# A split-precision encoder kernel on one core: the two parts of the activations put side by side in one tile

## Chip, core and metric

The kernel runs on one core of a Trainium2 chip. The metric is the device time of one execution in microseconds (us). "PE" is the matmul engine, "DVE" the vector engine, "ACT" the scalar engine, "POOL" GpSimd, "SP" the engine that here only issues DMAs.

## What is computed

Two residual layers over 256 tokens of width 2048, batch 1, float32 throughout. Cut to what matters:

```python
for layer in range(2):
    h = rms_norm(x, g[0])
    if layer % 2 == 0:                       # "even"
        proj = h @ even_w_in                 # GLA q, k, v, gate, 32 low-rank columns; neighbourhood attention q, k, v
        o = concat(gla_mixer(...), na_mixer(...))
        mix = o @ even_w_out
    else:                                    # "odd"
        proj = h @ odd_w_in                  # SSD z, x/B/C, 32 dt columns; sliding-window q, k, v
        o = concat(ssd_mixer(...), swa_mixer(...))
        mix = o @ odd_w_out
    x = x + rms_norm(mix, g[1])
    h = rms_norm(x, g[2])
    x = x + rms_norm((silu(h @ w_gate) * (h @ w_up)) @ w_down, g[3])
```

## The kernel before

**Split products.** Each float32 operand is split into a rounded part (hi, type fp32r) and the rest (lo). A product is then three matmuls: hi by hi, hi by lo, lo by hi; lo by lo is left out. Weights arrive over SP's DMA queue as halves of a chunk (`raw`, 128x1024, five buffers); for each half ACT makes `whi` (L184) and DVE makes `wlo` (L186), seven buffers each. The activations of a norm are transposed and split by `begin_norm` into four pairs of tiles `xth`, `xtl`, each 128 x 4 x 256 (four slices of the contraction, 256 tokens).

**Two kinds of product.** `unit_a` (L198) gives outputs with tokens on the partitions: activations are loaded into the array and 512 weight columns are streamed, 24 matmuls of 512 columns for a chunk and 128 tokens. `unit_b` (L233) gives transposed outputs: 128 weight columns are loaded, and the 256 tokens are streamed, 16 contraction steps of three matmuls of 256 columns. The even layer has 24 such units (GLA q and k: 8; attention q and k: 16), the odd layer 12 (the channels of the convolution, `conv`), and each layer one more of kind "L", for the 32 low-rank or dt columns: these stand in columns 0 to 15 and 32 to 47 of an otherwise zero chunk. The result of a unit stays in one of four PSUM tiles (`accb`) until a DVE multiplication by the row of norm factors (`mul_row`, L690 or L692) takes it out; L745 does so for the even layer's "L" unit, L1113 for the odd one's.

**What runs beside the units.** Mixers are generators (`spawn`, `tick`) that are stepped while the projections run. In the even layer `gla` turns the low-rank result `lrT` into decays (`gz`, L795) and then, for seven levels, forms `ge` on DVE and ACT, multiplies it (L845) and has PE make scores from it (`gs`, L821); DVE merges them (L851). The order of the instructions on each engine is set at compile time by the framework's scheduler; every engine then goes through its list in order.

**Memory.** Most 4 KB tiles come from one pool, `s4`, with 26 buffers: `xth` and `xtl` take 8 of them, the rest goes to residuals, mixer tiles, and, in the FFN, to the weights of its second product (`sw`, by SP's queue) and combinations of activations (`so`). The FFN's second product is done in fewer matmuls by adding weights and activations first (`quads`, L555; sums by L567; matmuls `sq`, L618 to L620). Before the end of each half layer, `post` has POOL load the residual `x` (L635) and the gains `gb` (L371).

Of the kernel before, what the change touches and what calls it, by code (L numbers as in the profile page):

```python
# [18 lines left out]
F32 = mybir.dt.float32  # L19
F32R = mybir.dt.float32r  # L20
# [19 lines left out]
PREP = 200  # L40
# [51 lines left out]
class Trunk:  # L92
    def __init__(self, tc, dr, out, stage=99):
        self.tc, self.nc, self.dr, self.out, self.stage = tc, tc.nc, dr, out, stage
        self.plan = []
        self.pending = deque()
        self.bg = []
        self.early = deque()
        self.hooks, self.mid = deque(), deque()
        self.lag = 2 * LAG  # L100
        self.nraw = 0
        self.rate, self.width, self.credit = 1.0, 3, 0.0
        self.n = 0
        self.pinned = {}
        self.pinning = ()
        self.ready = deque()
        self.tight = False
        self.splan, self.sraw, self.squeue = [], {}, deque()


# [50 lines left out]
    def chunk(self, kind, name, idx, k0, n0):  # L161

        if self.hooks and len(self.plan) == self.hooks[0][0]:
            self.hooks.popleft()[1]()
        self.plan.append((kind, name, idx, k0, n0))
        while len(self.ready) < 2:
            self.prep()
        n = 2 if kind == "A" else 8
        return [tuple(v.rearrange("p (k n) -> p k n", k=n) for v in self.ready.popleft()) for _ in range(2)]

    def prep(self):

        while len(self.early) < 4 and self.nraw < 2 * NCHUNK:
            self.load_half()
        if not self.early:
            return
        self.ready.append(self.halves(self.early.popleft()))

    def halves(self, src):

# [17 lines left out]
    def unit_a(self, chunks, xk, evac):  # L198

        nc = self.nc  # L200
        last = len(chunks) - 1
        ps = {}

        def part(t, ci, w, kt0, half):
            if ci == 0 and half == 0:
                ps[t] = self.pacc.tile([P, 512], F32, tag="acc", name=self.nm("acc"))
            for k in (2 * half, 2 * half + 1):
                wh, wl = w[half]
                xh, xl = xk(kt0 + k, t)
                s, e = ci == 0 and k == 0, ci == last and k == 3  # L210
                self.pin(nc.tensor.matmul(ps[t], xh, wh[:, k % 2], start=s, stop=False))  # L211
                self.pin(nc.tensor.matmul(ps[t], xh, wl[:, k % 2], start=False, stop=False))  # L212
                self.pin(nc.tensor.matmul(ps[t], xl, wh[:, k % 2], start=False, stop=e))  # L213
            if ci == last and half:
                evac(t, ps[t])
            self.tick(0.5)

        if self.tight:
            self.flush()
        for ci, (name, idx, k0, n0, kt0) in enumerate(chunks):  # L220
            w = self.chunk("A", name, idx, k0, n0)
            if self.tight:
                for half in range(2):
                    part(0, ci, w, kt0, half)
                    part(1, ci, w, kt0, half)
                continue
            for half in range(2):
                part(0, ci, w, kt0, half)
                if self.mid:
                    self.mid.popleft()()  # L230
            self.push(*(lambda h=h, ci=ci, w=w, kt0=kt0: part(1, ci, w, kt0, h) for h in range(2)))

    def unit_b(self, name, idx, n0, xt, kind="B"):  # L233

# [70 lines left out]
    def begin_norm(self, li, gi):  # L305

        nc = self.nc
        xt = ([None] * 4, [None] * 4)
        rs = [None, None]
        ssp = [None, None]  # L310
        gain = self.gT[:, li * 2 + gi // 2]

        def piece(t, j, src):
            if xt[0][j] is None:
                xt[0][j], xt[1][j] = self.slot([P, 4, T], F32R, "xth"), self.slot([P, 4, T], F32R, "xtl")
            if j == 0:
                ssp[t] = self.small([P, 4], "nss", "nss")
                rs[t] = self.keep.tile([P, 1], F32, tag="nrs", bufs=4, name=self.nm("nrs"))
            sl = slice(t * P, (t + 1) * P)
            hi, lo = xt[0][j][:, :, sl], xt[1][j][:, :, sl]  # L320
            with self.tc.high_priority(offset=NORM):
                ps = self.transpose4(src)
            yield
            with self.tc.high_priority(offset=NORM):
                gx = self.tmp([P, 4, P], nm="gx")
                self.pin(nc.vector.tensor_tensor(out=gx, in0=ps, in1=gain[:, 4 * j:4 * j + 4].unsqueeze(2)
                                                 .broadcast_to([P, 4, P]), op=ALU.mult))
                self.pin(nc.scalar.copy(hi, gx))  # L328
# [325 lines left out]
    def setup(self, ctx):  # L654
        nc, tc, dr = self.nc, self.tc, self.dr
        pool = lambda name, bufs, **k: ctx.enter_context(tc.tile_pool(name=name, bufs=bufs, **k))
        self.const = pool("const", 1)
        self.keep = pool("keep", 2)
        self.smp = pool("small", 8)
        self.raw = pool("raw", 5)  # L660
        self.whi = pool("whi", 7)
        self.wlo = pool("wlo", 7)
        self.s4 = pool("s4", 26)
        self.t2 = pool("t2", 4)
        self.t2m = pool("t2m", 6)
        self.junk = pool("junk", 1)
        self.pacc = pool("pacc", 4, space=PSUM)
        self.pmx = pool("pmx", 4, space=PSUM)
        self.dram = pool("dram", 1, space=bass.MemoryType.DRAM)
        self.xsrc = [self.dr["x"][t * P:(t + 1) * P] for t in range(2)]  # L670
        self.mhalf = self.const.tile([P, 1], F32, name="mhalf")
        nc.gpsimd.memset(self.mhalf, -0.5)
        self.load_const("ca", nc.scalar)
        self.x = [[None, None], [None, None]]
        self.load_x(0, 0, nc.sync)
        self.load_half()
        self.load_half()
# [47 lines left out]
    def even_mixers(self, norm, after):  # L725
        nc = self.nc
        self.have = {}
        self.in_xt, self.in_rs, _ = norm
        xt, w = self.in_xt, "even_w_in"
# [11 lines left out]
        nc.vector.tensor_copy(self.lv, lv)  # L741
        row = self.rstd_rows(self.in_rs)
        lrT = self.keep.tile([48, T], F32, tag="lrT", bufs=1, name="lrT")
        ps = self.unit_b(w, 0, 3072, xt, "L")
        nc.vector.tensor_mul(lrT, ps[0:48], row[0:48])  # L745
        for half in range(2):
            self.spawn(self.gla(half, lrT, mix))
        for half in range(2):
            t = self.slot([P, 2, 2, T], nm="gqk")
            for j in range(2):  # L750
                c0 = (2 * half + j) * P
                self.mul_row(t[:, 1, j], self.unit_b(w, 0, 512 + c0, xt), row)
                self.mul_row(t[:, 0, j], self.unit_b(w, 0, c0, xt), row, 0.125)
            self.have[f"qk{half}"] = t
        self.nat_unit(w, 1024, "gv0")
        self.nat_unit(w, 1024 + 512, "gv1")
# [1 line left out]
        for u in range(2):  # L758
            nq, nk = self.slot([P, 4, T], nm="nq"), self.slot([P, 4, T], nm="nk")
            for h in range(4):  # L760
                c0 = (4 * u + h) * P
                back = lambda x: x.rearrange("p (a t) -> p a t", a=2)[:, :, ::-1]
                self.mul_row(nq[:, h].rearrange("p (a t) -> p a t", a=2), back(self.unit_b(w, 0, 3104 + c0, xt)),
                             back(row), P ** -0.5)
                self.mul_row(nk[:, h], self.unit_b(w, 0, 4128 + c0, xt), row)
            self.nat_unit(w, 5152 + 512 * u, f"nv{u}")
            self.flush()
            self.new_mix(mix, 2 + u)
# [235 lines left out]
    def odd_mixers(self, norm, after):  # L1004
# [20 lines left out]
        self.unit_a([(w, 0, 512 * c, 3616, 4 * c) for c in range(4)], xk, ev_kv)  # L1025
        self.flush()
        row = self.rstd_rows(rs)
        ps = self.unit_b(w, 0, 2560, xt, "L")
        self.spawn(self.ssd_dt(ps, row))
        ssp = [self.small([P, 2], "yss", "yss") for _ in range(2)]  # L1030
        for g in range(2):
            bc = self.mtmp([P, 2, T], nm="bc")
# [68 lines left out]
            yield  # L1101
        return end

    def ssd_dt(self, ps, row):

        nc = self.nc
        R = 48

        def tl(nm):
            return self.mtmp([R, 2, T], nm=nm)  # L1110
        xu = tl("dx")
        x, u = xu[:, 0], xu[:, 1]
        nc.vector.tensor_mul(x, ps[0:R], row[0:R])  # L1113
        nc.scalar.activation(u, x, AF.Abs, bias=self.dtb[0:R])
        dt = self.keep.tile([R, T], F32, tag="lrT", bufs=1, name="dtk")
        nc.vector.tensor_scalar(out=dt, in0=x, scalar1=self.dtb[0:R], scalar2=0.0, op0=ALU.add, op1=ALU.max)
# [275 lines left out]
```

## Time and profile before

| | |
|---|---|
| time before, median of 3 runs | 2235.45 us (2234.25 to 2236.69) |
| the profiled execution's own time | 2236.18 us |
| its span in the profile | 2234.4 us, so 1.8 us lie outside |
| PE busy | 2189.1 us, 98% of the span |
| DVE busy | 1773.0 us |
| ACT busy | 1212.1 us |

A busy share is the union of an engine's instructions. A matmul's duration holds the time that its result needs to come out of the array, and the next one starts before that; how fast PE goes is read from the starts of neighbours, not from the durations.

### The profile page before, as it was taken

To read this page: it belongs to the slowest core of one execution; us is meant where nothing else is said; L and a number is where in the kernel's file an instruction comes from. 1 tells how busy PE (TensorE), PEld (TensorE's weight loads), DVE (VectorE), ACT (ScalarE), POOL (GpSimd) and SP (SyncE) were. 2 spreads that over 40 slices of the span, in tenths; PEclk is the share of its full clock that TensorE was granted. 3 is DMA by queue.
4 is the path that set the end of the run, shared out by engine and by line. 5 is a ranking of instruction groups with operands and counts; after the bars stand their busy time and mean duration, and the time that the engine had idled before them with its cause. 6 is when DMAs were issued, how large, how long until landed. Compare 5 with 4: busy or idle time off the path is not lost.

```text
span 2234.4 us, 29039 instructions
## 1 busy us (share of the span) xinstructions
PE 2189.1 (98%) x10888; PEld 1843.0 (82%) x10888; DVE 1773.0 (79%) x2134; ACT 1212.1 (54%) x1511; POOL 201.3 (9%) x246
## 2 busy tenths in 40 slices
PE   8999999999999999999989999999999999999997
PEld 7989998788888888888769988877888888888875
DVE  7877545766878888888989987766687889888896
ACT  6545345554555555555656545655556555555563
POOL 0001010210000000000021253121000000000002
PEclk9999999999999999999999999999999999999998
DMA  7445556575575655565656433657466565546563
GB/s 280 133 132 167 188 183 193 185 244 167 202 243 173 211 173 199 169 217 198 210 183 217 158 121 124 218 189 264 152 205 235 181 212 176 201 161 209 198 213 117
DMA packets 117325, 424.54 MB, mean 190 GB/s; under 512 B 13392, under 2 KB 13520, under 8 KB 117184
## 3 DMA queue, kind: packets, MB, share of 16 engines
q1 hardware_dynamic: 110592, 400.61, 53.4%
q0 software_dynamic: 6448, 21.99, 3.0%
q8 instruction: 85, 1.39, 0.2%
q14 instruction: 56, 0.46, 0.1%
q10 hardware_dynamic: 144, 0.10, 0.0%
HBM read 414.25 MB, written 8.39 MB: 189 GB/s over the span
## 4 chain that ended last, share of the span: by engine, by line
PE 88%; DVE 9%; issue 2%; DMA 1%; ACT 0%; POOL 0%; DVEq 0%; SPq 0%; ACTq 0%; POOLq 0%
PE acc L213 19%; PE acc L211 19%; PE acc L212 19%; PE sq L618 5%; PE sq L619 5%; PE sq L620 5%; DVE wlo L186 4%; PE accb L242 3%; PE accb L244 3%; PE accb L243 3%; DVE sw L567 1%; PE tp L285 1%; PE gs L821 1%; DVE f L627 1%; PE as L946 1%
## 5 line engine op out<-in xcount | busy, mean ns | idle before, releaser
L186 DVE TENSOR_TENSOR wlo<-raw,whi 128x1024 fp32r<-128x1024 f32 x596 | 741.7, 1252 | 292.4 <-ACT whi L184 284.5
L184 ACT CAST whi<-raw 128x1024 fp32r<-128x1024 f32 x596 | 624.5, 1051 | 580.6 <-PE acc L213 387.7
L213 PE MATMUL acc<-whi,xtl 128*128 128x512 f32 x1760 | 691.8, 394 | 6.0 <-DVE xtl L331 5.9
L212 PE MATMUL acc<-wlo,xth 128*128 128x512 f32 x1760 | 689.8, 393 | 0.6 <-DVE wlo L186 0.6
L211 PE MATMUL acc<-whi,xth 128*128 128x512 f32 x1760 | 677.3, 394 | 3.6 <-ACT xth L328 3.5
L184 ACT CAST whi<-sw 128x1024 fp32r<-128x1024 f32 x280 | 293.3, 1053 | 231.4 <-PE acc L213 132.6
L213 PEld LDWEIGHTS acc<-whi,xtl 128*128 128x128 f32 x1760 | 332.7, 189 | 77.6 <-DVE xtl L331 8.7
L211 PEld LDWEIGHTS acc<-whi,xth 128*128 128x128 f32 x1760 | 332.6, 189 | 73.9 <-ACT xth L328 5.4
L212 PEld LDWEIGHTS acc<-wlo,xth 128*128 128x128 f32 x1760 | 332.8, 189 | 70.8 <-DVE wlo L186 1.7
L186 DVE TENSOR_TENSOR wlo<-sw,whi 128x1024 fp32r<-128x1024 f32 x280 | 337.8, 1220 | 47.7 <-ACT whi L184 44.9
L619 PE MATMUL sq<-wlo,so 128*128 128x512 f32 x560 | 220.0, 393 | 4.5 <-DVE wlo L186 4.5
L620 PE MATMUL sq<-whi,so 128*128 128x512 f32 x560 | 219.2, 391 | 0.0
L618 PE MATMUL sq<-whi,so 128*128 128x512 f32 x560 | 219.2, 394 | 0.0
L567 DVE TENSOR_TENSOR sw<-sw,sw 128x1024 f32<-128x1024 f32 x160 | 193.8, 1220 | 17.9 <-DMA sw<-sstream 17.4
L242 PE MATMUL accb<-xth,whi 128*128 128x256 f32 x608 | 173.8, 286 | 0.0
L244 PE MATMUL accb<-xth,wlo 128*128 128x256 f32 x608 | 173.0, 285 | 0.0
L243 PE MATMUL accb<-xtl,whi 128*128 128x256 f32 x608 | 172.8, 284 | 0.0
L619 PEld LDWEIGHTS sq<-wlo,so 128*128 128x128 f32 x560 | 106.0, 189 | 28.6 <-DVE wlo L186 7.0
L620 PEld LDWEIGHTS sq<-whi,so 128*128 128x128 f32 x560 | 106.0, 189 | 22.5 <-DVE so L536 0.6
L618 PEld LDWEIGHTS sq<-whi,so 128*128 128x128 f32 x560 | 106.0, 189 | 22.2 <-ACT whi L184 0.4
L635 POOL DMA_DIRECT2D x<-xm x8 | 4.3, 544 | 1291.9 <-ACT whi L184 645.5
L242 PEld LDWEIGHTS accb<-xth,whi 128*128 128x128 f32 x608 | 116.5, 192 | 1.6 <-issue 0.7
(245 smaller groups left out, 2254.2 us busy)
## 6 DMA issues: line engine op xcount, KB each, us to landing
raw<-wstream SPq DMA_DIRECT2D x596, 512.0 KB, 4.9
sw<-sstream SPq DMA_DIRECT2D x160, 512.0 KB, 6.3
gb<-norm_gains POOLq DMA_DIRECT2D x16, 256.0 KB, 7.8
xm<-x POOLq DMA_DIRECT2D x16, 256.0 KB, 3.4
x<-xm POOLq DMA_DIRECT2D x8, 512.0 KB, 5.4
x<-x SPq DMA_DIRECT2D x4, 512.0 KB, 8.9
x<-x POOLq DMA_DIRECT2D x4, 512.0 KB, 7.7
xf<-x POOLq DMA_DIRECT2D x8, 256.0 KB, 3.2
```

The lines of the kernel that those rows point to most:

```text
L184: self.pin(nc.scalar.copy(hi, src))
L186: self.pin(nc.vector.tensor_sub(lo, src, hi.bitcast(F32)))
L211: self.pin(nc.tensor.matmul(ps[t], xh, wh[:, k % 2], start=s, stop=False))
L212: self.pin(nc.tensor.matmul(ps[t], xh, wl[:, k % 2], start=False, stop=False))
L213: self.pin(nc.tensor.matmul(ps[t], xl, wh[:, k % 2], start=False, stop=e))
L242: nc.tensor.matmul(ps, wh[:, kt % 8], xh, start=kt == 0, stop=False)
L243: nc.tensor.matmul(ps, wh[:, kt % 8], xl, start=False, stop=False)
L244: nc.tensor.matmul(ps, wl[:, kt % 8], xh, start=False, stop=kt == 15)
L567: nc.vector.tensor_add(a, a, b)
L618: nc.tensor.matmul(ps, xh, wh[:, k], start=s, stop=False)
L619: nc.tensor.matmul(ps, xh, wl[:, k], start=False, stop=False)
L620: nc.tensor.matmul(ps, xl, wh[:, k], start=False, stop=e)
```

## The change

The two parts of the activations become the two halves of one 8 KB tile, from a pool `s8` with four buffers; `s4` shrinks from 26 to 18 buffers. The even layer's 24 units become `unit_b2`: the product of `whi` with hi and with lo is one matmul of 512 columns, whose moving operand is two runs of 256 columns, 4 KB apart; the product of `wlo` with hi stays a matmul of 256 columns that adds into the first half. At the end ACT copies the second half out and DVE adds the first half to it, and the multiplication by the row follows. The odd layer's 12 units stay as they are. In the two "L" units the low parts of the 48 used columns are written into columns 64 to 111 of `whi` itself (`lhalf`), so that one matmul of 512 columns for each contraction step gives all products; two ACT copies, two DVE additions and the multiplication take the result out.

```diff
+LHALF = (9, 10, 323, 324)
...
+    def lhalf(self, src):
...
+            hi = self.whi.tile([P, 1024], F32R, tag="whi", name=self.nm("whi"))
+            self.pin(nc.scalar.copy(hi, src))
+            k, r = (v.rearrange("p (k n) -> p k n", k=8) for v in (hi, src))
+            self.pin(nc.vector.tensor_sub(k[:, :, 64:112], r[:, :, 0:48], k[:, :, 0:48].bitcast(F32)))
+        return hi, hi
...
+    def joined(self, kt, xt):
+        return xt[2][kt // 4][:, :, kt % 4, :]
+
+    def unit_b2(self, name, n0, xt):
...
+        ps = self.pacc.tile([P, 2, T], F32, tag="acc", name=self.nm("acc2"))
+        for kt in range(16):
+            wh, wl = w[kt // 8]
+            wide = lambda s, e: nc.tensor.matmul(ps, wh[:, kt % 8], self.joined(kt, xt), start=s, stop=e)
+            if kt < 15:
+                wide(kt == 0, False)
+            nc.tensor.matmul(ps[:, 0], wl[:, kt % 8], xt[0][kt // 4][:, kt % 4, :], start=False, stop=False)
+            if kt == 15:
+                wide(False, True)
...
+        t = self.tmp([P, T], nm="half")
+        nc.scalar.copy(t, ps[:, 1])
+        nc.vector.tensor_add(t, ps[:, 0], t)
+        return t
+
+    def unit_l(self, name, n0, xt, out, row):
...
+        for kt in range(16):
+            nc.tensor.matmul(ps, w[kt // 8][0][:, kt % 8], self.joined(kt, xt), start=kt == 0, stop=kt == 15)
...
+        t = self.tmp([48, 2, T], nm="lt")
+        nc.scalar.copy(t[:, 0], ps[0:48, 1])
+        nc.scalar.copy(t[:, 1], ps[64:112, 0])
+        nc.vector.tensor_add(t[:, 0], ps[0:48, 0], t[:, 0])
+        nc.vector.tensor_add(t[:, 0], t[:, 0], t[:, 1])
+        nc.vector.tensor_mul(out, t[:, 0], row[0:48])
...
-                xt[0][j], xt[1][j] = self.slot([P, 4, T], F32R, "xth"), self.slot([P, 4, T], F32R, "xtl")
+                xt[2][j] = self.s8.tile([P, 2, 4, T], F32R, tag="s8", name=self.nm("xt"))
+                xt[0][j], xt[1][j] = xt[2][j][:, 0], xt[2][j][:, 1]
...
-        self.s4 = pool("s4", 26)
+        self.s4 = pool("s4", 18)
+        self.s8 = pool("s8", 4)
...
-        ps = self.unit_b(w, 0, 3072, xt, "L")
-        nc.vector.tensor_mul(lrT, ps[0:48], row[0:48])
+        self.unit_l(w, 3072, xt, lrT, row)
...
-                self.mul_row(t[:, 1, j], self.unit_b(w, 0, 512 + c0, xt), row)
-                self.mul_row(t[:, 0, j], self.unit_b(w, 0, c0, xt), row, 0.125)
+                self.mul_row(t[:, 1, j], self.unit_b2(w, 512 + c0, xt), row)
+                self.mul_row(t[:, 0, j], self.unit_b2(w, c0, xt), row, 0.125)
```

PE, in a unit of the even layer's GLA q and k; `accb_474` is the unit's PSUM tile, each row one matmul. Before:

```order
L242 MATMUL accb_474<-xth_115,whi_464 128x256
L243 MATMUL accb_474<-xtl_116,whi_464 128x256
L244 MATMUL accb_474<-xth_115,wlo_466 128x256
L242 MATMUL accb_474<-xth_124,whi_464 128x256
L243 MATMUL accb_474<-xtl_125,whi_464 128x256
L244 MATMUL accb_474<-xth_124,wlo_466 128x256
```

Now, with `acc_94_444` the unit's tile, and `rb` the small matmuls that spread the norm factors:

```order
L257 MATMUL acc_94_444<-xt_126,whi_434 128x512
L260 MATMUL acc_94_444<-xt_126,wlo_436 128x256
L257 MATMUL acc_94_444<-xt_126,whi_434 128x512
L260 MATMUL acc_94_444<-xt_126,wlo_436 128x256
L401 MATMUL rb_389<-dg_390,ones 128x128
L401 MATMUL rb_389<-dg_393,ones 128x128
```

Three matmuls of a contraction step have become two, a wide and a narrow one by turns.

DVE, right behind the even layer's "L" unit: the norm row is copied, the low-rank result taken out, and weights and the first unit follow. Before:

```order
L346 COPY rstdB_389<-rb_390 128x256
L745 TENSOR_TENSOR lrT<-accb_411,rstdB_389 48x256
L186 TENSOR_TENSOR wlo_696<-raw_568,whi_694 128x1024
L186 TENSOR_TENSOR wlo_702<-raw_630,whi_700 128x1024
L798 TENSOR_SCALAR gm_499<-gz_501,cb_380 128x256
```

Now:

```order
L284 TENSOR_TENSOR lt_425<-accl_408,lt_425 48x256
L402 COPY rstdB_388<-rb_389 128x256
L285 TENSOR_TENSOR lt_425<-lt_425 48x256
L199 TENSOR_TENSOR wlo_633<-raw_574,whi_631 128x1024
L286 TENSOR_TENSOR lrT<-lt_425,rstdB_388 48x256
L199 TENSOR_TENSOR wlo_677<-raw_580,whi_675 128x1024
L267 TENSOR_TENSOR half_515<-acc_94_444,half_515 128x256
L199 TENSOR_TENSOR wlo_683<-raw_623,whi_681 128x1024
L854 TENSOR_SCALAR gm_461<-gz_463,cb_379 128x256
```

The low-rank result now needs three DVE instructions, with a `wlo` between them, and the addition of the first unit's halves stands ahead of the decays `gm`.

PE, where the scores of the second and third level of the first GLA half stand (`gs`, from `ge`). Before, inside the last q and k unit:

```order
L821 MATMUL gs_905<-ge_874 128x128 x4
L821 MATMUL gs_910<-ge_874 128x128 x4
L242 MATMUL accb_1011<-xth_115,whi_1001 128x256
L243 MATMUL accb_1011<-xtl_116,whi_1001 128x256
L244 MATMUL accb_1011<-xth_115,wlo_1003 128x256
L242 MATMUL accb_1011<-xth_115,whi_1001 128x256
L243 MATMUL accb_1011<-xtl_116,whi_1001 128x256
L821 MATMUL gs_986<-ge_955 128x128 x4
L821 MATMUL gs_991<-ge_955 128x128 x4
```

Now, behind that unit, in the projection for `gv0`:

```order
L226 MATMUL acc_958<-whi_992,xt_126 128x512
L877 MATMUL gs_794<-ge_771 128x128 x4
L877 MATMUL gs_799<-ge_771 128x128 x4
L877 MATMUL gs_862<-ge_839 128x128 x4
L877 MATMUL gs_867<-ge_839 128x128 x4
L224 MATMUL acc_958<-whi_992,xt_126 128x512
```

The scores have moved behind more of the projections. SP's list of DMAs is the same before and now, and PE's list in the FFN too.

## Rows read from the trace of the kernel before

**Rows 1.** The page: busy time, share and count by engine; PE's granted clock in 40 slices.

```profile
PE 2189.1 (98%) x10888; PEld 1843.0 (82%) x10888; DVE 1773.0 (79%) x2134; ACT 1212.1 (54%) x1511; POOL 201.3 (9%) x246
...
PEclk9999999999999999999999999999999999999998
```

**Rows 2.** The chain that ended last, shares by engine.

```profile
PE 88%; DVE 9%; issue 2%; DMA 1%; ACT 0%; POOL 0%; DVEq 0%; SPq 0%; ACTq 0%; POOLq 0%
```

**Rows 3.** Stretches: start:end us, length, busy us (count) by engine, clock, DMA.

```profile
47.00:130.00 83.00, 83.00 (x599) 74.92 (x598) 71.02 (x112) 48.46 (x56) 0.00 (x0) 1.00 0.39 125
...
1060.00:1100.00 40.00, 39.53 (x171) 31.45 (x170) 40.00 (x46) 23.22 (x26) 0.00 (x0) 1.00 0.63 209
```

**Rows 4.** Groups by line: count | busy us, mean ns | idle before, releaser.

```profile
L242 PE MATMUL accb<-xth,whi 128*128 128x256 f32 x608 | 173.8, 286 | 0.0
...
L821 PE MATMUL gs<-ge 64*128 64x128 f32 x256 | 24.9, 285 | 0.0
```

**Rows 5.** PE's timeline in a 256-column unit: start us, duration; 51 starts apart.

```profile
59.82 0.28 PE L244 MATMUL accb<-xth,wlo 128*128 128x256 f32 x1
...
65.94 0.28 PE L244 MATMUL accb<-xth,wlo 128*128 128x256 f32 x1
```

**Rows 6.** PE's timeline in a stretch of 512-column matmuls; 56 starts apart.

```profile
1699.70 0.39 PE L618 MATMUL sq<-whi,so 128*128 128x512 f32 x1
...
1712.40 0.39 PE L620 MATMUL sq<-whi,so 128*128 128x512 f32 x1
```

**Rows 7.** Groups by line, ACT and DVE: reads of 256 PSUM columns, weight halves.

```profile
L980 ACT CAST mixh<-apo 128x256 fp32r<-128x256 f32 x16 | 5.9, 372 | 10.0 <-PE apo L979 10.0
L981 DVE TENSOR_TENSOR mixl<-apo,mixh 128x256 fp32r<-128x256 f32 x16 | 6.6, 420 | 11.9 <-ACT mixh L980 11.7
L186 DVE TENSOR_TENSOR wlo<-raw,whi 128x1024 fp32r<-128x1024 f32 x596 | 741.7, 1252 | 292.4 <-ACT whi L184 284.5
```

**Rows 8.** DVE's timeline, 256-column operations back to back; 18 starts apart.

```profile
78.48 0.42 DVE L840 TENSOR_TENSOR ge<-gb 128x256 f32<-128x256 f32 x1
...
84.52 0.42 DVE L842 TENSOR_TENSOR ge<-gb 128x256 f32<-128x256 f32 x1
```

**Rows 9.** What DVE waited for, 47 to 130 us: us, times, longest.

```profile
DVE gat L851 <- PE gs L821: 4.8, 2, 3.8
DVE wlo L186 <- ACT whi L184: 4.4, 5, 1.7
DVE gm L803 <- ACT ga L802: 2.4, 2, 1.9
```

**Rows 10.** What ACT waited for, 20 to 340 us.

```profile
ACT whi L184 <- PE accb L243: 68.7, 39, 5.5
```

**Rows 11.** What PE waited for, whole span: its only waits for `wlo` in the FFN.

```profile
PE sq L619 <- DVE wlo L186: 4.5, 4, 1.8
```

**Rows 12.** Even FFN's end: timelines of SP, DVE, POOL; `sw` landing time (last number); `sq` first, last start.

```profile
1094.98 0.80 SPq L523 DMA_DIRECT2D sw<-sstream  x2
...
1110.79 1.22 DVE L567 TENSOR_TENSOR sw<-sw,sw 128x1024 f32<-128x1024 f32 x1
...
1108.76 1.12 POOL L635 DMA_DIRECT2D x<-xm  x2 [643.99 <-PE acc L213]
...
1157.30 1.57 POOL L410 TENSOR_SCALAR f<-f,prs 128x512 f32<-128x512 f32 x1
...
sw<-sstream SPq DMA_DIRECT2D x10, 512.0 KB, 5.4
...
L618 PE MATMUL sq<-whi,so x57: 387/389/775, 1041.2 to 1135.8; 128*128 128x512 f32 x57
```

**Rows 13.** POOL's timeline at the even layer's output projection.

```profile
331.93 0.53 POOL L635 DMA_DIRECT2D x<-x  x1 [23.51 <-PE acc L213]
360.97 0.54 POOL L371 DMA_DIRECT2D gb<-norm_gains  x1 [28.51 <-PE apt L969]
...
418.60 1.71 POOL L429 TENSOR_TENSOR f<-f,gb 128x512 f32<-128x512 f32 x1 [51.44 <-ACT sq L303]
```

More of the change, by code (lines that the diff above doesn't have):

```diff
@@ L106, in __init__ @@
         self.ready = deque()
-        self.tight = False
+        self.tight, self.nready = False, 0
         self.splan, self.sraw, self.squeue = [], {}, deque()
@@ L164, in chunk @@
             self.hooks.popleft()[1]()
+        assert (2 * len(self.plan) + 1 in LHALF) == (kind == "L"), len(self.plan)
         self.plan.append((kind, name, idx, k0, n0))
@@ L176, in prep @@
             return
-        self.ready.append(self.halves(self.early.popleft()))
+        self.nready += 1
+        self.ready.append((self.lhalf if self.nready in LHALF else self.halves)(self.early.popleft()))
+    def lhalf(self, src):
+        nc = self.nc
+        with self.tc.high_priority(offset=PREP):
+            hi = self.whi.tile([P, 1024], F32R, tag="whi", name=self.nm("whi"))
[3 more added lines that the diff above has]
+        return hi, hi
     def halves(self, src):
@@ L231, in unit_a @@
             self.push(*(lambda h=h, ci=ci, w=w, kt0=kt0: part(1, ci, w, kt0, h) for h in range(2)))
+    def joined(self, kt, xt):
+        return xt[2][kt // 4][:, :, kt % 4, :]
+    def unit_b2(self, name, n0, xt):
+        nc = self.nc
+        self.flush()
+        w = self.chunk("B", name, 0, 0, n0)
+        ps = self.pacc.tile([P, 2, T], F32, tag="acc", name=self.nm("acc2"))
[7 more added lines that the diff above has]
+                wide(False, True)
+            if kt % 8 == 7:
+                self.tick()
+        t = self.tmp([P, T], nm="half")
[3 more added lines that the diff above has]
+    def unit_l(self, name, n0, xt, out, row):
+        nc = self.nc
+        self.flush()
+        w = self.chunk("L", name, 0, 0, n0)
+        ps = self.pacc.tile([P, 2, T], F32, tag="acc", name=self.nm("accl"))
+        for kt in range(16):
+            nc.tensor.matmul(ps, w[kt // 8][0][:, kt % 8], self.joined(kt, xt), start=kt == 0, stop=kt == 15)
+            if kt % 8 == 7:
+                self.tick()
+        t = self.tmp([48, 2, T], nm="lt")
[4 more added lines that the diff above has]
+        nc.vector.tensor_mul(out, t[:, 0], row[0:48])
     def unit_b(self, name, idx, n0, xt, kind="B"):
@@ L307, in begin_norm @@
         nc = self.nc
-        xt = ([None] * 4, [None] * 4)
+        xt = ([None] * 4, [None] * 4, [None] * 4)
         rs = [None, None]
@@ L762, in even_mixers @@
                 back = lambda x: x.rearrange("p (a t) -> p a t", a=2)[:, :, ::-1]
-                self.mul_row(nq[:, h].rearrange("p (a t) -> p a t", a=2), back(self.unit_b(w, 0, 3104 + c0, xt)),
+                self.mul_row(nq[:, h].rearrange("p (a t) -> p a t", a=2), back(self.unit_b2(w, 3104 + c0, xt)),
                              back(row), P ** -0.5)
-                self.mul_row(nk[:, h], self.unit_b(w, 0, 4128 + c0, xt), row)
+                self.mul_row(nk[:, h], self.unit_b2(w, 4128 + c0, xt), row)
             self.nat_unit(w, 5152 + 512 * u, f"nv{u}")
@@ L1027, in odd_mixers @@
         row = self.rstd_rows(rs)
-        ps = self.unit_b(w, 0, 2560, xt, "L")
-        self.spawn(self.ssd_dt(ps, row))
+        xu = self.mtmp([48, 2, T], nm="dx")
+        self.unit_l(w, 2560, xt, xu[:, 0], row)
+        self.spawn(self.ssd_dt(xu))
         ssp = [self.small([P, 2], "yss", "yss") for _ in range(2)]
@@ L1102, in conv_end_x, with ssd_dt @@
         return end
-    def ssd_dt(self, ps, row):
+    def ssd_dt(self, xu):
         nc = self.nc
@@ L1110, in tl @@
             return self.mtmp([R, 2, T], nm=nm)
-        xu = tl("dx")
         x, u = xu[:, 0], xu[:, 1]
-        nc.vector.tensor_mul(x, ps[0:R], row[0:R])
         nc.scalar.activation(u, x, AF.Abs, bias=self.dtb[0:R])
```

## The prediction

> **What bounds the kernel now.** I read the page first, then the chain, then the stretches in which the changed units stand. The page shows PE busy for 98% of the span at full clock in all slices but the last [rows 1], and the chain that ended last runs over PE for 88%, over DVE for 9% [rows 2]. So a microsecond off PE is worth one only where DVE does not hold the chain. The stretches show both kinds: from 47 to 130 us, where the even layer's q and k units and the first GLA levels run, PE is busy all the time and DVE 71.0 of 83 us; from 1060 to 1100 us, at the end of the FFN, DVE is busy 40.0 of 40 us [rows 3]. The 256-column matmuls of the units never wait (idle 0.0), nor do the GLA scores [rows 4]. What paces them is therefore the step from one matmul to the next: in the timeline 51 starts take 65.94 - 59.82 = 6.12 us, **120.0 ns** each [rows 5]. The 512-column matmuls make 56 starts in 1712.40 - 1699.70 = 12.70 us, **226.8 ns** each [rows 6]. Two narrow ones cost 240.0 ns, 13.2 more than one wide one that streams as many columns; (226.8 - 120.0)/256 is 0.417 ns a column, which leaves a fixed part of 13.2 ns for each matmul.
>
> **The 24 even units.** Before, a unit is 48 steps of 120.0 ns = 5.76 us. Now it is 16 wide and 16 narrow ones. The narrow stays at 120.0. The wide one has a form that no row shows: 512 columns read in two runs. It can hardly cost less than the 226.8 of one run, and hardly more than the two instructions that read the same runs now, 240.0. I take 226.8, since 512 columns into one PSUM tile is what rows 6 time; the two runs only change addresses. Gain: 16 x 13.2 = 0.211 us a unit, 24 units: **5.07 us** (0 at the other bound).
>
> The Trainium skill, "TensorE: Matmul & The Clock Gate", section "Back-to-back issue gap", gives a step of N/2.4 + 2.5 ns: 109.2 for 256 columns and 215.8 for 512. By it the 24 units would gain only 24 x 16 x 2.6 ns = 1.0 us, and the two "L" units (48 narrow against 16 wide) 3.6 us, 4.6 in all. The rows do not agree: the fixed part is 13.2 ns, not 2.5 [rows 5, 6], and the sum goes by them.
>
> **The two "L" units.** 48 x 120.0 = 5.76 us become 16 x 226.8 = 3.63 us: 2.13 us each, **4.26 us** for two; at the other bound, 240.0, it is 3.84. Here columns are really saved (8192 streamed for 12288), so this part does not hang on the fixed part.
>
> **What is added beside PE.** Each even unit adds an ACT copy of 256 PSUM columns, by the nearest row 0.37 us, and a DVE addition, 0.42 us long [rows 7]; back to back such DVE operations step by (84.52 - 78.48)/18 = 0.336 us [rows 8]. The multiplication stays. ACT has room: its weight copies waited 68.7 us for PE to free a `whi` [rows 10], so a copy queued ahead of them eats such a wait; what queues behind it is `whi`, and PE would wait for that only if the wait ran out. The PSUM tile is held about a microsecond longer, with four tiles and a unit of 5.5 us. For an "L" unit the DVE's two half splits get shorter (48 of 128 columns), against two more additions and two ACT copies on 48 partitions. The even low-rank result comes 2 x 0.37 + 2 x 0.42 = 1.6 us later behind its unit, the unit ends 2.1 us earlier, and its first user `gz` stands several microseconds of matmuls behind. Priced at nothing.
>
> **DVE in 47 to 130 us** is the cover that could fail. It idles 83 - 71.0 = 12.0 us there [rows 3]. Now eight additions bring 8 x 0.336 = 2.7 us, and the stretch gets shorter by 8 x 0.211 = 1.7 us: 4.4 us less room. Of the idle time 4.8 us was DVE waiting for PE's scores, which is real slack, 4.4 us waiting for `whi` and 2.4 for ACT in the decays, which may not be given up [rows 9]. In-order lists make this sharper: the addition of a unit stands ahead of `gm` or `wlo` work, and if `ge` is late, `gs` holds PE and every projection matmul behind it. The new order moved `gs` back behind more projection matmuls, which is cover. The price lies between 0 (4.4 fits into 4.8) and 4.4 us (none does). I take one wait of the size that PE has for `wlo` where DVE is full, 4.5/4 = **1.1 us** [rows 11].
>
> **Eight buffers less in `s4`.** While the norm's tiles live, nothing changes: 26 - 8 = 18. Only where they are dead can other tiles run short. At the FFN's end the last pair of `sw` loads was issued at 1094.98 and first used at 1110.79, 15.8 us later, and lands in 5.4; `x` was issued at 1108.76, and the end of `post` that adds it begins at 1157.30 [rows 12]. A later buffer comes free with a product of `sq`: 56/4 = 14 products in 94.6 us, 6.8 us each, so the `sw` loads have 10.4 us to spare against some 7 that they may come later, and `x` far more. At the even output projection the fourth `x` load was issued at 331.93, the next POOL entry at 360.97, and `gb` is used at 418.60 [rows 13]: a delay of 20 us would be hidden. Price: nothing; if the cover is gone, the delay past 10.4 us, twice.
>
> **The sum.** 5.07 + 4.26 = 9.3 us off PE, 1.1 back: 8.2 us. The profiled execution took 2236.18 us (span 2234.4 and 1.8 outside) and would take 2228.0; the median of the runs lies 0.7 us below it, so the forecast is 2235.45 - 8.2 = **2227.2 us**. 0.2%, about what a measurement here can tell from no change, is 4.5 us: faster means under 2231.0.
>
> **The rivals.**
> - *Two runs cost two starts.* If the 13.2 ns belong to the start of a run of addresses, not to the instruction, the wide matmul takes 240.0 ns and the even units gain nothing: 3.8 us left, less 1.1, gives 2232.7. Against it: the same 13.2 ns stand on top of one run of 512 [rows 6]. For it: no row shows two runs. Chance 0.14.
> - *Only a fifth of the fixed part goes.* If most of the 13.2 ns does not go away with an instruction and only 2.6 ns does, the even units gain 384 x 2.6 ns = 1.0 us; an "L" unit keeps its saved columns, 4096 at 0.417 ns or 1.7 us, and gains 32 x 2.6 ns, 3.6 us for two: 4.6 us in all, 2230.9 before any wait. Against it: the two widths were timed with every matmul loading its own weights, as now, and 13.2 ns of it is not columns [rows 5, 6]. Chance 0.04. The skill's formula above comes to the same time.
> - *DVE takes the GLA stretch.* The full 4.4 us are lost: 2235.45 - 9.3 + 4.4 = 2230.5. For it: 86% busy before and in-order lists. Chance 0.12.
> - *Slower: the scores hold PE.* One chain of `gs` waits, repeated over the 14 level steps of both halves: `ge` late by one DVE weight split each, 1.25 us [rows 7], which nothing makes up, is 14 x 1.25 = 17.5 us. It turns the sign from 9.3 + 4.5 = 13.8 us on, one late split for eleven of the fourteen. 2235.45 - 9.3 + 17.5 = 2243.7. Against it: 12 us of DVE idle time, and no wait of `gs` before [rows 4]. Chance 0.06.
> - *Better than the sum:* no wait at all and the new order closes some of the gaps that PE has: 2226.1 or a little under, 0.05 for less than 2224.
>
> **Chances and range.** The forecast's own case, 2224 to 2230, holds 0.59; with the rivals 0.14, 0.04, 0.12, 0.06 and 0.05 that is all. Faster by over 0.2%: 0.59 + 0.05, two thirds of the DVE rival (0.08) and half of the formula's (0.02), and a little of the first where the 1.1 us stay away: 0.76. Within 0.2%: the rest of those and of the first rival, 0.18. Slower: 0.06. The range reaches from 2223.5 (the whole 9.3 and the runs' 1.2 us spread and a bit of luck with gaps) to 2233.0 (the first rival).
>
> **What would show it.** Right: the even units' matmuls start 227 and 120 ns apart by turns, "L" 227; 10 888 PE instructions become 24 x 16 + 2 x 32 = 448 fewer; PE's busy time falls by about as much as the span; PE's list of waits gains at most a microsecond or two on `wlo` or `ge` before 210 us; from 500 us to the end the FFNs take as long as before. Wrong: a wide start-to-start near 240; waits of `gs` or `go` for DVE of several microseconds; SP waiting so long for `sw` buffers near 1100 and 2160 us that DVE idles there.

## The result, and the profile after

The changed kernel takes **2223.79 us** (median of 6 runs, 2222.37 to 2225.77); the kernel before took 2235.53 us beside it. The ratio is 0.9948, 95% interval 0.9938 to 0.9958: faster by 0.5%, 11.7 us, where 8.2 us were forecast. The profiled execution took 2223.55 us, its span is 2221.7.

The page of the changed kernel: busy time by engine, PE's granted clock in 40 slices, and the chain that ended last.

```profile
PE 2177.6 (98%) x10440; PEld 1815.0 (82%) x10440; DVE 1776.4 (80%) x2162; ACT 1221.6 (55%) x1539; POOL 202.1 (9%) x246
...
PEclk9999999999999999999999999999999999999999
...
PE 88%; DVE 10%; issue 1%; ACT 0%; DMA 0%; POOL 0%; DVEq 0%; ACTq 0%; POOLq 0%
```

PE runs 448 instructions fewer and is busy 11.5 us less; DVE and ACT are busier by 3.4 and 9.5 us. The bound is where it was [rows 1, 2].

The two stretches of [rows 3] in the changed kernel (columns as there), and the wide matmuls' group:

```profile
47.00:130.00 83.00, 83.00 (x480) 68.85 (x479) 73.58 (x120) 52.50 (x65) 0.00 (x0) 0.98 0.38 128
1060.00:1100.00 40.00, 38.19 (x160) 30.82 (x160) 40.00 (x43) 20.28 (x23) 0.00 (x0) 0.96 0.67 220
```
```profile
L257 PE MATMUL acc<-xt,whi 128*128 128x512 f32 x384 | 137.1, 402 | 0.0
```

Between 47 and 130 us DVE has 2.6 us more work in the same 83 us, and PE still never waits. In the changed program L257 is the wide matmul, L260 the narrow one behind it, L278 that of an "L" unit. PE's timeline in two neighbouring even units and in the even "L" unit (start us, duration; an "xN" row holds N of them):

```profile
294.32 0.39 PE L257 MATMUL acc<-xt,whi 128*128 128x512 f32 x1
294.55 0.28 PE L260 MATMUL acc<-xt,wlo 128*128 128x256 f32 x1
...
296.40 0.39 PE L257 MATMUL acc<-xt,whi 128*128 128x512 f32 x1
```
```profile
297.44 0.40 PE L257 MATMUL acc<-xt,whi 128*128 128x512 f32 x1
...
298.85 0.40 PE L257 MATMUL acc<-xt,whi 128*128 128x512 f32 x1
```
```profile
35.25 3.79 PE L278 MATMUL accl<-xt,whi 128*128 128x512 f32 x16
```

A step (one wide, one narrow) takes (296.40 - 294.32)/6 = 347 ns in the first unit, as 226.8 + 120.0 predicts, but (298.85 - 297.44)/4 = 353 ns in the second. Before it was 3 x 120.0 = 360. These two kinds of unit come back below. The "L" unit's 16 starts lie (3.79 - 0.39)/15 = 227 ns apart.

What PE waited for, whole span (us in total, times, longest):

```profile
PE acc L226 <- DVE xt L387: 7.6, 7, 1.9
PE tp L340 <- DVE h L522: 7.1, 2, 3.5
...
PE sq L675 <- DVE wlo L199: 4.5, 4, 1.8
PE tp L340 <- DVE x L469: 3.8, 4, 1.4
```

No wait for the scores or for `ge` has appeared, and `sq` waits for `wlo` as before [rows 11].

**A ledger.** PE's order of weight halves is the same in both kernels, so the start of the first matmul on a given half can be subtracted, before minus this kernel; what grows from one place to the next was gained in between. Two such places of the even layer, the third weight half of its first projection and the first of its output projection that reads the attention results, in the timelines of before, after, and a second execution of after (the experiment "again"):

```profile
15.75 0.39 PE L211 MATMUL acc<-whi,xth 128*128 128x512 f32 x1
...
345.29 0.39 PE L211 MATMUL acc<-whi,mixh 128*128 128x512 f32 x1
```
```profile
14.41 0.39 PE L224 MATMUL acc<-whi,xt 128*128 128x512 f32 x1
...
338.54 0.39 PE L224 MATMUL acc<-whi,mixh 128*128 128x512 f32 x1
```
```profile
15.42 0.39 PE L224 MATMUL acc<-whi,xt 128*128 128x512 f32 x1
...
338.00 0.39 PE L224 MATMUL acc<-whi,mixh 128*128 128x512 f32 x1
```

The stretch takes 329.54 us before, 324.13 after and 322.58 in the second execution of the very same program. All places, as gain in us against the profile of before (time of the place in before at the left; names as in the experiments below):

| place, us in before | after | again | even L only | pools | units | L units | two narrow | sorted | conv | DVE x5 |
|---|---|---|---|---|---|---|---|---|---|---|
| 15.75, first projection | 1.3 | 0.3 | 0.3 | 0.9 | 0.5 | 1.0 | 1.2 | 1.4 | 0.9 | 1.7 |
| 345.29, even output projection | 6.8 | 7.3 | 7.2 | 0.9 | 2.0 | 1.7 | 1.1 | 7.9 | 6.4 | 5.6 |
| 486.13, even FFN | 8.0 | 8.6 | 8.5 | 0.9 | 3.3 | 1.7 | 2.4 | 9.2 | 7.6 | 6.8 |
| 1177.45, odd first projection | 10.9 | 9.7 | 9.5 | 0.4 | 3.1 | 1.9 | 2.4 | 8.7 | 7.6 | 8.2 |
| 1461.56, odd output projection | 11.8 | 10.9 | 8.9 | -0.4 | 2.2 | 4.2 | 4.9 | 10.3 | 6.0 | 9.2 |
| end of the span | 12.7 | 10.7 | 9.8 | 0.5 | 3.1 | 5.4 | 5.9 | 11.6 | 7.3 | 10.2 |

### The profile page after: what moved, and what is told of

Same layout as the page of the kernel before. It is cut to its first block, busy times and chain, and to the rows that moved or that the text cites. A ratio compares the mean times of both kernels' runs of the same rounds, so it can differ in the third digit from the quotient of the medians.

```text
span 2221.7 us, 28237 instructions
## 1 busy us (share of the span) xinstructions
PE 2177.6 (98%) x10440; PEld 1815.0 (82%) x10440; DVE 1776.4 (80%) x2162; ACT 1221.6 (55%) x1539; POOL 202.1 (9%) x246
## 4 chain that ended last, share of the span: by engine, by line
PE 88%; DVE 10%; issue 1%; ACT 0%; DMA 0%; POOL 0%; DVEq 0%; ACTq 0%; POOLq 0%
PE acc L225 19%; PE acc L226 19%; PE acc L224 19%; PE sq L675 5%; PE sq L674 5%; PE sq L676 5%; DVE wlo L199 4%; PE acc L257 4%; PE acc L260 2%; DVE sw L623 1%; PE tp L340 1%; PE accb L298 1%; PE gs L877 1%; PE accb L297 1%; PE accb L299 1%
## 5 line engine op out<-in xcount | busy, mean ns | idle before, releaser
L199 DVE TENSOR_TENSOR wlo<-raw,whi 128x1024 fp32r<-128x1024 f32 x592 | 732.0, 1243 | 289.8 <-ACT whi L197 283.0
L226 PE MATMUL acc<-whi,xt 128*128 128x512 f32 x1760 | 690.2, 393 | 7.6 <-DVE xt L387 7.6
L225 PE MATMUL acc<-wlo,xt 128*128 128x512 f32 x1760 | 689.1, 393 | 0.1
L224 PE MATMUL acc<-whi,xt 128*128 128x512 f32 x1760 | 677.3, 393 | 3.2 <-ACT xt L384 3.1
L226 PEld LDWEIGHTS acc<-whi,xt 128*128 128x128 f32 x1760 | 332.5, 189 | 78.8 <-DVE xt L387 10.2
L224 PEld LDWEIGHTS acc<-whi,xt 128*128 128x128 f32 x1760 | 332.3, 189 | 73.6 <-ACT xt L384 5.2
L225 PEld LDWEIGHTS acc<-wlo,xt 128*128 128x128 f32 x1760 | 332.7, 189 | 69.7 <-DVE wlo L199 0.6
L257 PE MATMUL acc<-xt,whi 128*128 128x512 f32 x384 | 137.1, 402 | 0.0
L260 PE MATMUL acc<-xt,wlo 128*128 128x256 f32 x384 | 105.6, 285 | 0.0
L224 PE MATMUL acc<-whi,mixh 128*128 128x512 f32 x256 | 97.7, 396 | 0.0
L226 PE MATMUL acc<-whi,mixl 128*128 128x512 f32 x256 | 97.5, 390 | 0.0
```

Of the source, the lines that this page charges most:

```text
L199: self.pin(nc.vector.tensor_sub(lo, src, hi.bitcast(F32)))
L257: wide = lambda s, e: nc.tensor.matmul(ps, wh[:, kt % 8], self.joined(kt, xt), start=s, stop=e)
L260: nc.tensor.matmul(ps[:, 0], wl[:, kt % 8], xt[0][kt // 4][:, kt % 4, :], start=False, stop=False)
```

## The experiments

Theory: the gain is the sum of the parts that the prediction names, corrected in size, and the 3.5 us that it lacked are order and clock (PE's granted clock falls to half, 1.2 GHz, for some microseconds at a time: "half clock" below). Rival: the pool split makes the scheduler write the FFNs' ends differently, where the first profile gains 2.9 us between 486 and 1177 us.

**Pools alone (e1_pools).** The kernel before, with the joined tiles but every unit as before:

```diff
+                xt[2][j] = self.s8.tile([P, 2, 4, T], F32R, tag="s8", name=self.nm("xt"))
-        self.s4 = pool("s4", 26)
+        self.s4 = pool("s4", 18)
+        self.s8 = pool("s8", 4)
```

> The kernel before with one thing of the change: the split activations lie in four 8 KB tiles of a pool of their own, and `s4` has 18 buffers; all units multiply as before. Parts theory (even units 24 x 16 x 10 ns = 3.8 us by the step of 350 ns seen after, L units 4.3 us, pools nothing, the rest of the 11.7 us granted clock): 2235.5 us, between 2234 and 2237, the first use of every weight half within 1 us of before up to the last FFN. Order theory (the buffer split alone makes the scheduler write another order at the FFNs' ends, which is where 2.9 and 0.9 us were gained after): 2231.7 us, with 2 to 3 us gained between 1060 and 1180 us and about 1 us after 2150 us.

2235.87 us, ratio 0.9999 [0.9991, 1.0008]. The rival falls. The ledger loses 0.8 us between the odd layer's first projection and its output projection, as "units" (0.9) and "even L only" (0.6) do too: a small cost of the pools at that norm. All of it stands in the steps of the `acc` matmuls (160.4 us there, 159.6 before), and no stretch at half clock lies there; PE's listed waits explain part of it (`acc` for the lower activation parts 6.4 us in the whole span against 5.9).

**The even units alone (e2_units).**

```diff
-LHALF = (9, 10, 323, 324)
+LHALF = ()
-        self.unit_l(w, 3072, xt, lrT, row)
+        ps = self.unit_b(w, 0, 3072, xt, "L")
+        nc.vector.tensor_mul(lrT, ps[0:48], row[0:48])
...
```

> The change without its L units: the 24 even units are wide and narrow by turns, the two L units run as 48 narrow matmuls as before. Parts theory: 2235.5 - 3.8 = 2231.7 us, and the L halves take 5.76 us again. Order theory: the 3.9 us of the FFNs' ends come on top, 2227.8 us. If the even units gained nothing by themselves (two runs cost two starts), 2235.5 us.

2231.72 us, ratio 0.9984 [0.9975, 0.9993]: 4.0 us, the parts theory's number.

**The L units alone (e3_lunits).**

```diff
-                self.mul_row(t[:, 1, j], self.unit_b2(w, 512 + c0, xt), row)
+                self.mul_row(t[:, 1, j], self.unit_b(w, 0, 512 + c0, xt), row)
...
```

> The change without its wide even units: those run as 48 narrow matmuls as before, the two L units stack weight parts. Parts theory: 2235.5 - 4.3 = 2231.2 us; 2.1 us of it at the even L unit, and 2.1 us at the odd one, where the ledger of after shows only 0.9 net. If the odd L unit's gain is eaten again by what follows it (the gain after it is 0.9): 2232.5 us. Order theory: 2227.5 us.

2231.39 us, ratio 0.9981 [0.9972, 0.9990]: 4.4 us for 4.26 predicted. But 4.0 + 4.4 is 8.4, not 11.7; with intervals of 2 us each way, 3.3 us too little is no more than a hint.

**Two narrow ones for a wide one (e4_twonarrow).**

```diff
-            wide = lambda s, e: nc.tensor.matmul(ps, wh[:, kt % 8], self.joined(kt, xt), start=s, stop=e)
+            def wide(s, e):
+                if s or e:
+                    nc.tensor.matmul(ps, wh[:, kt % 8], self.joined(kt, xt), start=s, stop=e)
+                    return
+                for p in range(2):
+                    nc.tensor.matmul(ps[:, p], wh[:, kt % 8], xt[p][kt // 4][:, kt % 4, :], start=False, stop=False)
```

> The changed kernel, where in 14 of the 16 steps of an even unit the wide matmul is again two narrow ones into the two halves of the same PSUM tile, with the same copy and addition behind it. Instruction theory (what an even unit gains is the fixed part of the instruction that falls away): a step is 360 ns instead of 350, 24 x 14 x 10 ns = 3.4 us are lost again, 2227.2 us. Rival (the gain comes from order and clock, and the wide form is worth nothing): 2223.8 us, as after.

2230.82 us, ratio 0.9979 [0.9970, 0.9988]: 7 us slower than after, so the wide form is worth something, though twice the number expected. Between the ledger's first two places its units' steps add up to 143.5 us against after's 139.2; the profile has 6.8 us of half clock there and after 3.4. Scores and decays take 23.89 and 4.08 us, as long as before or longer (after: 23.37 and 2.94), so part of the 7 us is order and clock, not the wide form.

**One run (e5_onerun).**

```diff
+            run = xt[0][kt // 4][:, kt % 4 // 2 * 2:kt % 4 // 2 * 2 + 2, :]
-            wide = lambda s, e: nc.tensor.matmul(ps, wh[:, kt % 8], self.joined(kt, xt), start=s, stop=e)
+            wide = lambda s, e: nc.tensor.matmul(ps, wh[:, kt % 8], run, start=s, stop=e)
```

> The changed kernel, where the wide matmuls of the 24 even units read one contiguous run of 512 columns (two neighbouring slices of the upper parts) in place of two runs; the product of the upper weights with the lower activations is left out by that. After showed units of two kinds, with steps (wide and narrow together) of about 348 and of about 353 ns, where 226.8 + 120.0 make 346.8. If the second run costs the difference, every step becomes 347 ns: 24 units gain 0.21 us each instead of 0.11 to 0.20, about 1.2 us in all, 2222.6 us. If it is the turn from wide to narrow or something else, both kinds stay and the time is that of after, 2223.8 us.

2223.44 us, ratio 0.9948 [0.9935, 0.9962], and both kinds of unit are there, half by half as in after (uninterrupted halves take 2.775 to 2.838 us for eight steps in both, and the same half agrees to 1 ns outside the half clock). The second run costs nothing.

**Sorted (e6_sorted).**

```diff
+            if kt % 8 == 7:
+                for k in range(kt - 7, kt + 1):
+                    nc.tensor.matmul(ps[:, 0], wl[:, k % 8], xt[0][k // 4][:, k % 4, :], start=False, stop=False)
-            nc.tensor.matmul(ps[:, 0], wl[:, kt % 8], xt[0][kt // 4][:, kt % 4, :], start=False, stop=False)
```

> The changed kernel, where an even unit runs the eight wide matmuls of a weight half first and then its eight narrow ones, in place of taking turns. If the turn from wide to narrow costs the few nanoseconds above 346.8, a half becomes 8 x 346.8 = 2774 ns in every unit (after: 2777 to 2837 ns), 1.2 us less in all, 2222.6 us; if the two runs or something outside the unit cost it, the halves stay as they are, 2223.8 us.

2224.32 us, ratio 0.9953 [0.9940, 0.9965]: no better. Where nothing cuts in, its halves take 2.787 and 2.800 us by turns, so the two kinds are gone: they belong to taking turns. But the best unit of after takes 5.56 us and each of these 5.59, so sorting does not reach 2 x 2.774 either. Between the ledger's first two places its units' steps add up to 136.4 us, 1.3 less than the 137.7 of the second execution of after and about the 1.2 expected; but the scores, in another order, take 24.96 us in place of 23.37. So the time does not show that sorting is worth nothing.

**Convolution units too (e7_conv).**

```diff
-        ps = self.unit_b("odd_w_in", 0, 1024 + c * P, xt)
+        ps = self.unit_b2("odd_w_in", 1024 + c * P, xt)
```

> The changed kernel, where the 12 convolution units of the odd layer are also wide and narrow by turns, with the copy and the addition behind them. If the instruction's fixed part is all that counts and DVE's additional 12 x 0.336 = 4.0 us lie beside PE: 12 x (0.11 to 0.20) = 1.3 to 2.4 us less, 2221.9 us. Rival (the odd layer is where each unit is followed by a chain of DVE work that PE's transposes wait for): the additions delay these, no gain or up to 4 us lost, 2224 to 2228 us.

2228.32 us, ratio 0.9968 [0.9957, 0.9980]: **4.5 us slower than after**. The 12 units' own steps add up to 68.2 us for 70.1, the predicted gain. What PE waited for between 1300 and 1440 us, where after waits for nothing, and the stretch of that wait (busy time by engine, clock):

```profile
PE apo L1035 <- DVE mxv L1004: 1.3, 1, 1.3
PE yp L1281 <- POOL seg L1275: 0.7, 2, 0.4
PE apt L1025 <- DVE sc L1018: 0.6, 1, 0.6
PE as L1002 <- DVE mxv L1004: 0.3, 1, 0.3
```
```profile
1402.40:1405.80 3.40, 3.05 (x9) 2.29 (x10) 2.61 (x14) 1.77 (x7) 0.00 (x0) 0.51 0.01 2
```

PE reaches the end of the projections earlier, the maxima and scores that DVE makes for the attention, and the `seg` that POOL makes, do not, and PE stands still for 2.9 us; among these waits lies a stretch of 3.4 us at half clock (0.51) that after does not have. By the ledger, taken from the odd layer's first projection to the middle of its FFN (1177 to 1811 us in before), this kernel loses 2.9 us where after gains 0.9: 3.9 us of the 4.5. That is the rival's outcome.

**More DVE work (e8_dve4).**

```diff
+        for _ in range(4):
+            nc.vector.tensor_add(self.tmp([P, T], nm="dup"), ps[:, 0], t)
         nc.vector.tensor_add(t, ps[:, 0], t)
```

> The changed kernel with four more DVE additions of the same size, to a scratch tile, ahead of the one that each even unit got: 32 x 0.336 = 10.8 us more DVE work in the eight q and k units before 130 us, where DVE was idle for 83 - 73.6 = 9.4 us, and 21.5 us in the other sixteen. If all of that idle time is cover: about 1.4 us lost, 2225.2 us. If only DVE's waits for PE are cover, as the prediction argued for its upper bound, about 10 us lost, with PE waiting for lower weight parts or for the scores, 2234 us. If PE has enough other matmuls to run ahead: nothing, 2223.8 us.

2225.99 us, ratio 0.9959 [0.9946, 0.9971]: 2.2 us slower than after, for 32 us of DVE work. The stretch, and PE's only wait from 47 to 345 us (after has none):

```profile
47.00:130.00 83.00, 83.00 (x461) 68.74 (x460) 77.68 (x145) 49.92 (x62) 0.00 (x0) 0.98 0.41 135
```
```profile
PE gs L935 <- DVE gat L909: 0.6, 1, 0.6
```

By the ledger (first to second place) after gained 5.4 us and this 3.9, a loss of 1.5, close to the 1.4 expected if all of DVE's idle time is cover. All 32 additions of the q and k units lie in this stretch; DVE's groups there, the additions, then the seven products `ge` here and the eleven in after:

```profile
L268 DVE TENSOR_TENSOR dup<-acc,half 128x256 f32<-128x256 f32 x32 | 12.7, 420 | 0.0
L903 DVE TENSOR_TENSOR ge<-ge,gqk 128x1024 f32<-128x1024 f32 x7 | 8.5, 1221 | 0.0
```
```profile
L901 DVE TENSOR_TENSOR ge<-ge,gqk 128x1024 f32<-128x1024 f32 x11 | 13.3, 1221 | 0.0
```

DVE is only 4.1 us busier (77.7 for 73.6 us), and 5.3 us of idle time are left: the rest of the room came from mixer work that moved behind 130 us, which cost PE little.

**The same kernel again (e9_again).** No edit.

> The changed kernel itself, profiled a second time. If the stretches at half clock, the start and the waits are this program's own, they stand where they stood (57, 439, 1095, 1160, 1494, 2149, 2184 and 2214 us) and the ledger of first uses agrees with the first profile to 0.1 us throughout. If they are a matter of the single execution, the matmuls' steps and the order agree to the nanosecond between stretches, while other stretches come and go, each worth 1.7 us for 3.4 us at half clock, and the time lies anywhere from 2222 to 2226 us.

2223.66 us, ratio 0.9948 [0.9936, 0.9960]: the gain repeats. The stretches at half clock do not. The clock around 57 us, after first, then again:

```profile
54.00:64.00 10.00, 10.00 (x46) 7.74 (x43) 7.32 (x11) 9.54 (x12) 0.00 (x0) 0.83 0.25 81
57.00:60.40 3.40, 3.40 (x13) 2.92 (x12) 1.45 (x3) 3.37 (x4) 0.00 (x0) 0.51 0.07 29
```
```profile
54.00:64.00 10.00, 10.00 (x53) 7.47 (x52) 7.18 (x11) 8.89 (x13) 0.00 (x0) 1.00 0.18 61
```

A stretch of 3.4 us at the lower level (0.51 of 2.4 GHz, so 1.2 GHz) costs 324.13 - 322.58 = 1.55 us. Elsewhere in that part the two executions agree step by step.

**Even L alone (e10_evenl).** After, with the odd layer's L unit as before:

```diff
-LHALF = (9, 10, 323, 324)
+LHALF = (9, 10)
-        self.unit_l(w, 2560, xt, xu[:, 0], row)
-        self.spawn(self.ssd_dt(xu))
+        ps = self.unit_b(w, 0, 2560, xt, "L")
+        self.spawn(self.ssd_dt(ps, row))
```

> The changed kernel, where the L unit of the odd layer alone runs as 48 narrow matmuls as before. Parts theory: 2.1 us more than the changed kernel, 2225.9 us. If what the odd L unit saves is taken back by waits or clock behind it: 2223.8 to 2224.7 us. If the 11.7 us hang on the program as a whole (its order, and the stretches at half clock that follow from it), the time falls back towards the sum of the parts, 2228 us or more.

2226.74 us, ratio 0.9960 [0.9946, 0.9974]: 3.1 us above "again". The odd layer in "again", then here, from its first projection to its output projection:

```profile
1167.78 0.39 PE L224 MATMUL acc<-whi,xt 128*128 128x512 f32 x1
...
1450.70 0.39 PE L224 MATMUL acc<-whi,mixh 128*128 128x512 f32 x1
```
```profile
1167.94 0.39 PE L223 MATMUL acc<-whi,xt 128*128 128x512 f32 x1
...
1452.65 0.39 PE L223 MATMUL acc<-whi,mixh 128*128 128x512 f32 x1
```

282.92 against 284.71 us: the odd L unit gains 1.8 of its 2.13 us there. The other 1.3 of the 3.1 us are not explained; they lie within the intervals, 3 us each way.

## Why the prediction was right, and where its sizes were off

The time lies inside the range and on the forecast side, but 3.4 us under the forecast, at 2223.79 just inside the case "better than the sum" (under 2224, chance 0.05) and only 0.3 us above the range's lower end: no wait at all, and a new order that closes gaps. That is what happened as far as the gain is explained, and the forecast's own case missed it by the sizes below. The direction and the parts were foreseen; that the time still fell inside the range was partly luck, since the forecast did not have the gains of 1.1 and 1.3 us below and 2.4 us are not settled at all. What should show it did: 448 instructions fewer, PE's busy time 11.5 us less for 12.7 us of span, no new waits, and a ledger that stays at 8.0 us from 486 to 1081 us, through most of the even FFN.

**The 24 even units**: the mechanism held, the term was too big. 3.7 us instead of 5.07: in "again" their steps between the ledger's first two places add up to 91.4 (wide) + 46.2 (narrow) = 137.7 us, and with the L unit's 3.6 to 141.3, against 147.15 before for the 25 units; less the L unit's 2.13 that leaves 3.7. In the units of the first kind a step does cost 347 ns, as 226.8 + 120.0 gives (by the starts 230 and 117); in the others it costs 353. "One run" shows that the two runs of addresses are not what it is, "sorted" that it belongs to taking turns. The traces show what sorts the units: in "again" each unit that starts right behind one that ended at 353 ns a step goes on at 353 (8 of 8), and 347 is found only from a place on where other small matmuls (`rb`, `gz`, `gs`, `go`, `tp`, `as`, `apt`, `apo`) have cut in, to the end of that unit or of the next. Why the engine keeps to either step stays open; no experiment changed the cuts alone. The rival in which two runs cost two starts falls, and so does the one in which only a fifth of the fixed part goes (1.0 us). By that formula of the Trainium skill ("TensorE: Matmul & The Clock Gate", section "Back-to-back issue gap"), which the section gives for a matmul by itself and says not to hold in a stream of weight loads and matmuls, a step would have been 215.8 + 109.2 = 325 ns. No uninterrupted half of a unit in after was under 2.775 us, 347 ns a step.

**The two L units**: 4.26 us predicted; 2.1 us (even) by its steps and 1.8 us (odd) by the ledger, 4.4 us measured for both alone.

**ACT and DVE beside PE; the 1.1 us for DVE's cover**: the additions cost PE no wait, and the price was not paid. PE waits neither for `wlo` nor for scores before 345 us, and not for the later low-rank result. The step that was off is the bound: the prediction counted 4.8 of DVE's 12.0 us of idle time as safe, the waits for PE's scores. With five additions for one, DVE idled 5.3 us, so it had given up 6.7, and the loss over the whole even part was 1.5 us in the ledger for some 32 us of added work: waits for ACT were cover too, and mixer work could move later. The rivals "DVE takes the GLA stretch" (4.4 us) and "the scores hold PE" (17.5 us) fall: not even five additions cost that.

**The buffers of `s4`**: nothing, as priced, in the time (0.9999); 0.8 us at the odd norm by the ledger.

**What the sum lacked.** Two gains that no term had:
- *GLA groups, 1.1 us.* Scores and decays run in small groups between projection matmuls, and going in and out of a group costs PE extra steps. Taken from the starts before and in "again": the 256 scores took 23.90 and 23.37 us, the 16 decays 3.56 and 2.94. The decays that leave the group go to the next matmul after 304 ns; there were five such exits before and are four now, and the scores' exits of 202 ns fell from 11 to 10. Two groups of decays before, and in "again" the one of four that stands in their place:

```profile
50.51 0.69 PE L795 MATMUL gz<-lrT,cb 16*128 16x256 f32 x2
...
51.45 0.69 PE L795 MATMUL gz<-lrT,cb 16*128 16x256 f32 x2
```
```profile
54.58 0.70 PE L851 MATMUL gz<-lrT,cb 16*128 16x256 f32 x4
```

  "Units" and "L units" keep 23.90, and 3.56 or 3.67: the new order came only with both parts together, and explains 1.1 us of what 4.0 + 4.4 lacks.
- *The even norm, 1.3 us.* PE's waits for the residual between 415 and 490 us, before, then after:

```profile
PE tp L285 <- DVE x L413: 1.8, 2, 1.3
```
```profile
PE tp L340 <- DVE x L469: 0.5, 1, 0.5
PE tp L340 <- POOL x L467: 0.2, 1, 0.2
```

  The ledger gains 1.2 to 1.3 us there in every kernel with the new even units: in "units", which has no half clock there, and in "two narrow", which has 6.8 us of it like before. So it is the wait, not the clock. DVE's timeline shows why the residual's addition ends earlier; two weight splits, the residual and the next norm's first product, before, then in "again":

```profile
435.54 5.74 DVE L186 TENSOR_TENSOR wlo<-raw,whi 128x1024 fp32r<-128x1024 f32 x2
441.20 0.74 DVE L413 SCALAR_TENSOR_TENSOR x<-f,prs,x 128x512 f32<-128x512 f32 x1
441.86 0.68 DVE L326 TENSOR_TENSOR gx<-tp,ca 128x512 f32<-128x512 f32 x1
```
```profile
428.29 3.44 DVE L199 TENSOR_TENSOR wlo<-raw,whi 128x1024 fp32r<-128x1024 f32 x2
431.65 1.78 DVE L469 SCALAR_TENSOR_TENSOR x<-f,prs,x 128x512 f32<-128x512 f32 x1
433.36 0.68 DVE L382 TENSOR_TENSOR gx<-tp,ca 128x512 f32<-128x512 f32 x1
```

  From the first `wlo` to `gx` it is 6.32 us, then 5.07: 1.25 us less. One of the two `wlo` takes 4.61 us in before, "pools" and "L units", and none over 2.31 in all kernels with the new even units. Beside them POOL multiplies by `gb` and adds to the residual in all of these kernels; what makes one `wlo` so long is not settled.

So the ledger of "again" shows 7.0 us up to the even output projection (3.7 + 2.1 + 1.1 and 0.1 of small steps), 1.3 at the even norm and 1.2 in the odd layer (1.8 less the pools' cost): 9.4 us, for 9.3 predicted without the wait, but of other parts. That the two agree is luck: the even units were put 1.4 us too high, the L units 0.4, the pools 0.6 too low in cost, and 2.4 us of gains had no term. The runs' medians differ by 11.7 and 11.9. **The last 2.4 us are not settled.** They lie at the starts and the FFNs' ends, where profiles of one program differ: the two of after by 1.0 us at the first place, and between 486 and 1177 us by 1.8. Half of the length of all stretches at half clock is 18.4 us before, 18.9 to 21.8 in "pools", "units", "L units", "two narrow" and "conv", and 14.0 to 16.7 in after, "again", "even L only", "one run", "sorted" and "DVE x5". That fits, but part of it lies where PE waits for DVE, and no experiment changed the clock alone.

## What to carry to other kernels

Joining two narrow matmuls that read the same weights is worth the fixed part of one instruction, 3.7 us/384 = 10 ns each here; columns that are no longer streamed are worth far more (2 us for an L unit, against 0.15 for an even one, which streams as many as before). A unit that gains on PE gives it back when the next thing PE needs hangs on a DVE chain: the same edit that gained in the even layer cost 3.9 us in the odd one, though its matmuls there took 1.9 us less. To judge a change of this size, subtract the starts of the same instruction in two traces place by place, and profile the same program twice before explaining a difference of 2 us.

## What the runs showed of the hardware

- The same sequence of wide and narrow matmuls runs at 347 or 353 ns a step without any wait. Which of the two follows from what ran before it: 353 goes on from unit to unit, and 347 comes only after other matmuls have cut in ("again").
- A 512-column operand read in two runs of 256 paces like one run: 2.775 to 2.838 us for eight steps with either ("one run" and after).
- From the last decay of a group to the next projection matmul 304 ns pass, between two decays up to 320, where projection matmuls of one form follow each other after 120.0 or 226.8.
- Stretches at half clock differ between two executions of one program (eight in after, six in "again"); one of 3.4 us under busy PE costs 1.55 us.
- At the even norm one of two equal `wlo` splits takes 4.61 us in before and its neighbour 1.21; in "again" the two take 2.31 and 1.21.
